# A recurrent mixer rewritten without a reciprocal, in pairs of blocks, with its gate weights as two ordinary weight tiles

## The chip, the cores and the metric

The kernel runs on one core of one Trainium2 chip. The metric is device microseconds of one execution. The kernel before takes 1469.25 us, the median of three runs from 1468.46 to 1470.31.

## The reference

Two layers of a decoder trunk for one prompt (16 learned tokens and 512 of its own) and eight samples of eight tokens. Layer 0 is stick-breaking attention beside a multi-scale pooling, layer 1 a recurrent block; each layer ends in a gated FFN with a convolution of width 3, and each half is followed by `x <- LN(alpha*x + f(x))`. The change lies in the recurrent block, with 1024 channels in 8 blocks of 128:

```
gate, rec = split(x @ lru_w_in)
xc        = causal depthwise conv of width 4 over rec, plus bias
gate_r    = sigmoid(xc @ w_a + b_a)           per block of 128 channels
gate_i    = sigmoid(xc @ w_x + b_x)
log_a     = -8 * gate_r * softplus(-lambda);  a = exp(log_a)
b         = sqrt(-expm1(2*log_a)) * gate_i * xc;   b[0] += a[0] * h0
h[t]      = a[t] * h[t-1] + b[t]              a scan over time
out       = (gelu(gate) * h) @ lru_w_out
```

## The kernel before

Activations lie with channels on partitions and all 592 tokens along the free axis: 528 of the prompt (`TP`), then 8 samples of 8. A product in full precision is three float32r matmuls: of high parts, of low part and high part, and the other way round (`mm3`, L121). So each weight tile is loaded by DMA into `wraw` (two buffers), copied on ScalarE to its high part and subtracted on VectorE or GpSimd to its low part (`split` at L98, `weights` at L105). `whl` tiles come in turn from two pools of three. Activations that feed matmuls are split in the same way: `ch`/`cl` of the convolution's result, `yh`/`yl` of the mixer's result, always copied on ScalarE and subtracted on GpSimd. Tokens are worked in two chunks of 296 (`CH`).

The recurrent mixer is written block by block. `rec_c` (L905) multiplies for `rec` and evacuates into `re`, `gate_c` (L918) for `gate` with gelu into `gt`. `conv4` (L929) makes `xc` in four steps on VectorE, a tensor_scalar and three products of two tensors, and splits it. `lru` (L949) loads and splits this block's 128x256 gate weights (`gr`, `wga`), multiplies (`pga`, 12 matmuls), takes sigmoids into `rg` and `ig`, and then works without an exponential. With t the Tanh of half the exponent's size, a = 2/(1+t) - 1, and the root is sqrt(t) * 2/(1+t):

```
act.activation(rg, rg, AF.Tanh, scale=sc4[:, i:i + 1])
dve.tensor_scalar(aa, rg, 1.0, None, op0=OP.add)
dve.reciprocal(aa, aa)
act.activation(rg, rg, AF.Sqrt)
```

The scan (L983) runs over all tokens at once. At each sample's first token a is set to 0 and a*h0 added to b, by three operations of 8 elements. `fin` (L989) multiplies by the gate and splits to `yh`/`yl`.

The string `ORDER` (L38) lists the pieces: r is `rec_c` and `conv4`, g is `gate_c`, B is `lru`, o one block of the first part of the output projection (`lru_out`, tiles `plo`, from the y of blocks 0 to 2). A block's `fin` follows when its B and its g are there. Five pieces (`seq`, L995) have their first chunk multiplied earlier, while the second chunk of the layer norm before is still being made. Behind the ORDER comes the second part of the projection (`Residual` with `w_lo1`, tiles `pr`, from the y of blocks 3 to 7, 15 matmuls for each of 8 output blocks and 2 chunks), whose statistics and norm lead into the second FFN.

Each engine runs its instructions in one fixed order. In this part a scheduler sets the orders when the program is built, from the order as written, its own cost model and the buffers that are free; so they do not stand in the source. Tiles with tag "e" (`et`, 8 buffers) hold `re`, `rt`, `rg`, `ig`, `aa` and `gt`; `blk` tiles (19) hold `xc` among others. TensorE's results go to six banks of PSUM (`pd`), which are free again when ScalarE has read them.

Of the kernel before, what the change touches and what calls it, by code (L numbers as in the profile page):

```python
# [10 lines left out]
F32 = mybir.dt.float32  # L11
# [8 lines left out]
KB = 8  # L20
# [17 lines left out]
ORDER = 'r0 r1 r2 g0 B0 r3 B1 g1 r4 B2 g2 r5 B3 g3 r6 B4 g4 r7 B5 g5 B6 g6 B7 g7 o0 o1 o2 o3 o4 o5 o6 o7'  # L38
# [6 lines left out]
HQ, EP = 19, 8  # L45
# [3 lines left out]
BW = 3 + TP + NS * 11  # L49

# [18 lines left out]
def trunk(ctx: ExitStack, tc: tile.TileContext, I, O):  # L69
# [35 lines left out]
    def weights(src, nk, le=None, parts=1, between=None):  # L105

        raw = wp.tile([128, 1024], F32, tag="wraw", name="wraw", bufs=2)
        wpool, tag = wcfg["pools"][wcfg["n"] % len(wcfg["pools"])]
        wcfg["n"] += 1
        w = wpool.tile([128, 2, 1024], F32R, tag=tag, name="whl")  # L110
        step = nk * 128 // parts
        for i in range(parts):
            wcfg["dma"].dma_start(raw[:, i * step:i * step + step], src[:, i * step:i * step + step])
# [804 lines left out]
    def gate_c(i, w, ci):  # L918
        lo, hi = CH[ci]
        p = pd("pgt", hi - lo)  # L920
        mm3(p, w, xh, xl, lo, hi, KB, 0, 4)
        yield
        mm3(p, w, xh, xl, lo, hi, KB, 4, 8)
        if ci == 0:
            gts[i] = et(f"gt{i}", n=T)
        act.activation(gts[i][:, lo:hi], p, AF.Gelu_apprx_tanh)
        yield

    def conv4(i):  # L929
# [10 lines left out]
        xc = blk(f"xc{i}")  # L940
        dve.scalar_tensor_tensor(xc[:, :TP], e[:, 3:3 + TP], cws[3], t[:, :TP], op0=OP.mult, op1=OP.add)
        tv = t[:, 3 + TP:3 + TP + NS * (TS + 3)].rearrange("p (s n) -> p s n", s=NS)[:, :, :TS]
        dve.scalar_tensor_tensor(xc[:, TP:].rearrange("p (s n) -> p s n", s=NS), ev[:, :, 3:], cws[3], tv,
                                 op0=OP.mult, op1=OP.add)
        ch, cl = pairA("c", i)
# [3 lines left out]
    def lru(i):  # L949
        xc, ch, cl = xcs.pop(i)  # L950
# [16 lines left out]
        aa = et(f"aa{i}", n=T)
# [210 lines left out]
```

## Time and profile before

| | us |
|---|---|
| median of three runs | 1469.25 |
| the profiled execution | 1470.56 |
| its span, first to last instruction | 1468.8 |
| busy: TensorE | 1371.5 (93%) |
| busy: VectorE | 816.1 (56%) |
| busy: ScalarE | 587.3 (40%) |
| busy: GpSimd | 451.2 (31%) |
| mean granted TensorE clock | 0.97 of full speed |

The profile is one execution, taken by the hardware profiler. PE is TensorE, DVE is VectorE, ACT is ScalarE, POOL is GpSimd. L949 is a line of the kernel. A share over the whole span mixes stages: attention up to some 390 us, the two FFNs, and the recurrent mixer from about 776 to 970 us. A granted clock of 1.00 is 2.4 GHz, the lower level is 1.2 GHz.

### The profile page before, as it was taken

The page shows a single profiled execution, that of the slowest core. Times are in us where ns is not written, and L with a number is a line of the kernel's source. Part 1 is how long each engine was busy: PE and PEld are TensorE (multiplying, and loading weights), DVE is VectorE, ACT ScalarE, POOL GpSimd, SP SyncE. Part 2 cuts the span into 40 slices and gives each one's busy share as a digit, 9 for nine tenths or more (in the row PEclk, how much of TensorE's full clock was granted, in tenths as well). Part 3 has the DMA queues.
Part 4 walks back from the last instruction along what each step waited for, and adds up shares of the span by engine and source line. Part 5 has one row for each costly group of instructions (what it writes and reads, how often), then busy time and mean ns, then how long its engine had stood idle before and what let it go on. Part 6 is the DMA issues. An engine that isn't in the chain of part 4 may idle for free.

```text
span 1468.8 us, 26738 instructions
## 1 busy us (share of the span) xinstructions
PE 1371.5 (93%) x10491; PEld 1294.3 (88%) x10491; DVE 816.1 (56%) x1220; ACT 587.3 (40%) x1083; POOL 451.2 (31%) x621
## 2 busy tenths in 40 slices
PE   8999798998999999999997787897999999999995
PEld 7988555798999999999997787886999999999994
DVE  4226676575743344334477699888734344433456
ACT  4333575444522233213245466735522133312333
POOL 3112220346320011102257656447531012101244
PEclk9999899999999999999998898998999999999997
DMA  9499887842422222222241210143222222222121
GB/s 311 169 373 372 308 286 259 302 135 87 129 73 87 86 73 87 79 80 79 67 120 58 62 65 28 28 121 115 73 91 82 87 81 78 87 87 87 57 90 65
DMA packets 78592, 183.74 MB, mean 125 GB/s; under 512 B 9458, under 2 KB 18291, under 8 KB 78467
## 3 DMA queue, kind: packets, MB, share of 16 engines
q1 hardware_dynamic: 75362, 170.77, 35.3%
q0 software_dynamic: 3104, 11.27, 2.1%
q8 instruction: 83, 1.36, 0.4%
q14 instruction: 43, 0.34, 0.1%
HBM read 176.38 MB, written 5.62 MB: 124 GB/s over the span
## 4 chain that ended last, share of the span: by engine, by line
PE 75%; DVE 14%; issue 4%; ACT 3%; POOL 2%; DMA 1%; SPq 0%; DVEq 0%; ACTq 0%; POOLq 0%
PE pv L127 19%; PE pg L127 18%; PE pdn L127 14%; PE pr L127 4%; PE pqk L127 3%; PE zs L640 2%; PE pv L415 2%; DVE r L251 2%; PE av L668 2%; DVE whl L101 2%; PE zp L517 1%; PE pu L127 1%; DVE r L250 1%; PE prc L127 1%; DVE r L209 1%
## 5 line engine op out<-in xcount | busy, mean ns | idle before, releaser
L100 ACT ACTIVATE whl<-wraw 128x1024 fp32r<-128x1024 f32 (+4 forms) x217 | 212.4, 981 | 338.9 <-PE pdn L127 150.6
L127 PE MATMUL pg<-xh,whl 128*128 128x296 f32 (+1 forms) x1408 | 293.0, 300 | 4.2 <-ACT xh L257 4.2
L101 DVE TENSOR_TENSOR whl<-wraw,whl 128x1024 fp32r<-128x1024 f32 (+3 forms) x198 | 234.9, 1187 | 102.2 <-ACT whl L100 101.6
L127 PE MATMUL pv<-xh,whl 128*128 128x296 f32 (+1 forms) x1408 | 290.2, 298 | 0.0
L127 PEld LDWEIGHTS pg<-xh,whl 128*128 128x128 f32 x1408 | 231.5, 191 | 4.8 <-ACT xh L257 4.4
L127 PEld LDWEIGHTS pv<-xh,whl 128*128 128x128 f32 x1408 | 229.0, 188 | 0.0
L127 PE MATMUL pg<-xl,whl 128*128 128x296 f32 (+1 forms) x704 | 210.7, 301 | 6.8 <-POOL xl L258 6.8
L127 PE MATMUL pv<-xl,whl 128*128 128x296 f32 (+1 forms) x704 | 209.1, 297 | 0.0
L127 PE MATMUL pdn<-fh,whl 128*128 128x296 f32 (+1 forms) x1024 | 207.7, 298 | 0.0
L101 POOL TENSOR_TENSOR fl<-f,fh 128x592 fp32r<-128x592 f32 (+1 forms) x44 | 82.7, 1879 | 273.1 <-ACT fh L100 273.1
L127 PEld LDWEIGHTS pdn<-fh,whl 128*128 128x128 f32 x1024 | 165.5, 188 | 0.0
L127 PE MATMUL pdn<-fl,whl 128*128 128x296 f32 (+1 forms) x512 | 151.7, 297 | 0.0
L127 PEld LDWEIGHTS pg<-xl,whl 128*128 128x128 f32 x704 | 133.8, 191 | 9.0 <-POOL xl L258 8.9
L127 PEld LDWEIGHTS pv<-xl,whl 128*128 128x128 f32 x704 | 133.0, 189 | 0.0
L807 DVE TENSOR_SCALAR gc<-ge,sm 128x608 f32<-128x608 f32 x44 | 26.2, 595 | 169.4 <-ACT ge L770 159.4
L801 POOL COPY fout<-ge 128x2 f32<-128x2 f32 x44 | 15.7, 358 | 326.1 <-ACT ge L767 326.0
L767 ACT ACTIVATE ge<-pg 128x296 f32<-128x296 f32 (+2 forms) x88 | 33.8, 386 | 157.2 <-PE pg L127 155.2
L127 PEld LDWEIGHTS pdn<-fl,whl 128*128 128x128 f32 x512 | 96.4, 189 | 0.0
L393 DVE TENSOR_TENSOR_SCAN kp<-kp,zero 128x256 f32<-128x256 f32 (+5 forms) x70 | 54.1, 774 | 73.7 <-ACT kp L392 73.2
L864 DVE SCALAR_TENSOR_TENSOR r<-r,pdn 128x296 f32<-128x296 f32 (+1 forms) x64 | 29.0, 459 | 118.0 <-PE pdn L127 118.0
L821 DVE TENSOR_TENSOR f<-gc,pv 128x296 f32<-128x296 f32 (+1 forms) x88 | 37.5, 426 | 99.6 <-PE pv L127 75.4
L127 PE MATMUL pr<-fh,whl 128*128 128x296 f32 (+1 forms) x384 | 79.4, 300 | 0.0
(263 smaller groups left out, 2726.9 us busy)
## 6 DMA issues: line engine op xcount, KB each, us to landing
ck<-in_ck SPq DMA_DIRECT2D x128, 256.0 KB, 5.1
cv<-in_cv SPq DMA_DIRECT2D x128, 256.0 KB, 5.2
wraw<-in_w_g SPq DMA_DIRECT2D x44, 512.0 KB, 3.3
wraw<-in_w_vv SPq DMA_DIRECT2D x44, 512.0 KB, 3.4
wraw<-in_w_d SPq DMA_DIRECT2D x32, 512.0 KB, 3.3
wraw<-in_w_d SPq DMA_DIRECT2D x26, 384.0 KB, 3.1
wraw<-in_w_lo SPq DMA_DIRECT2D x13, 320.0 KB, 3.0
wraw<-in_w_o POOLq DMA_DIRECT2D x8, 512.0 KB, 6.4
```

Source lines behind the costliest of these rows:

```text
L100: act.activation(h, src, AF.Copy)
L101: (le or dve).tensor_tensor(l, src, h.bitcast(F32), op=OP.subtract)
L127: pe.matmul(ps, lhsT=w[:, wi, s], rhs=x[k][:, lo:hi], start=(n == 0), stop=(n == 3 * nk - 1))
L251: dve.scalar_tensor_tensor(x, x, g, rs, op0=OP.mult, op1=OP.mult)
L393: dve.tensor_tensor_scan(kp[:, n - 1::-1], kp[:, n - 1::-1], zero.to_broadcast([128, n]), 1.0 if carry is None else carry, op0=OP.mult, op ...
L415: pe.matmul(p, lhsT=x[k][:, i * 128:i * 128 + n], rhs=w[k // 4][:, wi, s], start=(j == 0), stop=(j == 3 * KB - 1))
L640: pe.matmul(z[c * 32:c * 32 + 32, :256].rearrange("p (j n) -> p j n", j=2), lhsT=qb[b][:, c, r, :], rhs=kt[:, b, :, c * 128:c * 128 + 128] ...
L668: pe.matmul(av[c * 32:c * 32 + 32], lhsT=an[:, j * 128 + c * 32:j * 128 + c * 32 + 32], rhs=vt[:, :, j, c * 128:c * 128 + 128], start=(u = ...
L767: act.activation(e[:, k + lo:k + z], p[:, :z - lo], AF.Copy)
L807: dve.tensor_scalar(t[:, :n], e[:, :n], cws[0], smc("fcb", L * FB + j), op0=OP.mult, op1=OP.add)
L821: dve.tensor_tensor(f[:, lo:z], t[:, lo:z], p[:, :z - lo], op=OP.mult)
L864: dve.scalar_tensor_tensor(x, x, ALPHA if gi == 0 else 1.0, p, op0=OP.mult, op1=OP.add)
```

## The change

- The coefficient a is taken with Exp, and one correction step takes up Exp's error: with w from Exp and t from Tanh, nt = (w+1)t + (w-1), nt = (w+1)nt, a = w - nt/2. The root is sqrt(t) * (1+a). The reciprocal and its two tensor_scalars are gone; four 600-wide products of two tensors a block come in (L991 to L994 of the new file), and one Exp on ScalarE.
- The first step of the width-4 convolution goes from VectorE to ScalarE (an Identity activation with scale and bias, L944).
- Each sample has a column of its own for its start: tiles are 600 wide (`XW`), a is 0 there and b is h0. One memset and one copy of 8 elements replace the three operations at the starts; the gate product becomes two pieces (528 and 64 wide); `pga` is worked in two halves of 300.
- `lru` takes two blocks: all their sigmoids, then both Exp, both Tanh, then each block's rest.
- The gate weights of four blocks become one ordinary weight tile: w0 stands ahead of everything in ORDER, w1 ahead of r6. Eight small loads and splits go.
- ORDER is rewritten in pairs (B01, B23, B45, B67). `seq` has four r and one g where it had three r and two g. "e" tiles: 13 where there were 8. `xc` moves to an "e" tile, `gt` to a `blk` tile.

```
-ORDER = 'r0 r1 r2 g0 B0 r3 B1 g1 r4 B2 g2 r5 B3 g3 r6 B4 g4 r7 B5 g5 B6 g6 B7 g7 o0 ... o7'
+ORDER = 'w0 r0 r1 r2 r3 g0 B01 g1 r4 r5 g2 B23 g3 w1 r6 r7 g4 B45 g5 g6 B67 g7 o0 ... o7'
-HQ, EP = 19, 8
+HQ, EP = 19, 13
+XW = TP + NS * (1 + TS)
+CX = ((0, XW // 2), (XW // 2, XW))
...
-        dve.tensor_scalar(t[:, :n], e[:, :n], cws[0], smc("lcb", i), op0=OP.mult, op1=OP.add)
+        act.activation(t[:, :n], e[:, :n], AF.Identity, scale=cws[0], bias=smc("lcb", i))
...
-    def lru(i):
-        raw = w2.tile([128, 256], F32, tag="gr", name="gr", bufs=1)
-        sp.dma_start(raw, I["w_ga"][i])
-        wga = w2.tile([128, 2, 256], F32R, tag="wga", name="wga", bufs=1)
-        split(wga[:, 0], wga[:, 1], raw)
...
-        act.activation(rg, rg, AF.Tanh, scale=sc4[:, i:i + 1])
-        dve.tensor_scalar(aa, rg, 1.0, None, op0=OP.add)
-        dve.reciprocal(aa, aa)
-        act.activation(rg, rg, AF.Sqrt)
-        pool.tensor_tensor(ig, ig, xc, op=OP.mult)
-        dve.scalar_tensor_tensor(rg, rg, 2.0, aa, op0=OP.mult, op1=OP.mult)
-        dve.tensor_tensor(ig, ig, rg, op=OP.mult)
-        dve.tensor_scalar(aa, aa, 2.0, -1.0, op0=OP.mult, op1=OP.add)
...
+    def lru(ids):
...
+        for i in ids:
+            w = ws[i] = et(f"aa{i}", n=XW)
+            act.activation(w, rgs[i], AF.Exp, scale=sc8[:, i:i + 1])
+        for i in ids:
+            act.activation(rgs[i], rgs[i], AF.Tanh, scale=sc4[:, i:i + 1])
+        for i in ids:
+            w, rg, ig = ws[i], rgs[i], igs[i]
+            xc = xcs.pop(i)[0]
+            pool.tensor_tensor(ig, ig, xc, op=OP.mult)
+            t = et(f"nt{i}", n=XW)
+            dve.scalar_tensor_tensor(t, w, 1.0, rg, op0=OP.add, op1=OP.mult)
+            dve.scalar_tensor_tensor(t, w, -1.0, t, op0=OP.add, op1=OP.add)
+            dve.scalar_tensor_tensor(t, w, 1.0, t, op0=OP.add, op1=OP.mult)
+            dve.scalar_tensor_tensor(w, t, -0.5, w, op0=OP.mult, op1=OP.add)
+            act.activation(rg, rg, AF.Sqrt)
+            dve.scalar_tensor_tensor(rg, w, 1.0, rg, op0=OP.add, op1=OP.mult)
+            dve.tensor_tensor(ig, ig, rg, op=OP.mult)
+            dve.memset(starts(w), 0.0)
+            dve.tensor_copy(starts(ig), smr("h0")[:, i * 8:i * 8 + 8].rearrange("p (s n) -> p s n", n=1))
+            dve.tensor_tensor_scan(ig, w, ig, 0.0, op0=OP.mult, op1=OP.add)
...
+        elif k == "w":
+            wgas[i] = weights(I["w_ga"][i * 4:i * 4 + 4].rearrange("b p n -> p b n"), KB)
```

What the scheduler makes of it is seen in the queues. The first place is ScalarE between the sigmoids and the Sqrt. Before, this is block 1 (`rg_9434` and `ig_9435` are its gates, `re_9533` is block 4):

```order
L964 ACT_TABLE_LOAD
L964 ACTIVATE rg_9434<-pga,sm 128x296 x2
L100 ACTIVATE wga<-gr 128x256
L966 ACTIVATE rg_9434<-rg_9434,sc_8907 128x592
L926 ACT_TABLE_LOAD
L926 ACTIVATE gt_9125<-pgt 128x296
L100 ACTIVATE whl<-wraw 128x1024
L964 ACT_TABLE_LOAD
L964 ACTIVATE ig_9435<-pga,sm 128x296 x2
L767 ACTIVATE re_9533<-prc 128x296
L970 ACT_TABLE_LOAD
L970 ACTIVATE rg_9434<-rg_9434 128x592
```

After the change, between the pairs 01 and 23 (`ch_9654` is of block 5, `rg_9716` and `ig_9717` of block 2, `rg_9738` and `ig_9739` of block 3, `gt_9688` of block 2); behind these rows stand a weight split, a table load, the Exp of block 3 and the Tanh of block 2:

```order
L102 ACTIVATE ch_9654<-xc_9650 128x600
L933 ACTIVATE gt_9688<-pgt 128x296
L102 ACTIVATE whl<-wraw 128x1024
L978 ACT_TABLE_LOAD
L978 ACTIVATE rg_9716<-pga,sm 128x300 x2
L978 ACTIVATE ig_9717<-pga,sm 128x300 x2
L978 ACTIVATE rg_9738<-pga,sm 128x300 x2
L978 ACTIVATE ig_9739<-pga,sm 128x300
L983 ACT_TABLE_LOAD
L983 ACTIVATE aa_9760<-rg_9716,sc_8937 128x600
L978 ACT_TABLE_LOAD
L978 ACTIVATE ig_9739<-pga,sm 128x300
```

The sigmoids of two blocks stand together, but the last one comes behind a first Exp, and the copy of block 5's convolution stands ahead of them all. The queue has 28 table loads between the mixer's first gelu and its last in the old program, and 32 in the new one.

The second place is VectorE at the same point. Before, it begins with the scan of block 0 (L983, which this list names like any product) and the reciprocal of block 1 (`aa_9457`); `ig_9313` is block 0, `rt_9566` and `re_9533` block 4, `rg_9434` block 1:

```order
L983 SCALAR_TENSOR_TENSOR ig_9313<-aa_9335,ig_9313 128x592
L969 RECIPROCAL aa_9457<-aa_9457 128x592
L991 TENSOR_TENSOR ig_9313<-ig_9313,gt_9078 128x592
L937 TENSOR_SCALAR rt_9566<-re_9533,sm 128x616
L101 TENSOR_TENSOR wga<-gr,wga 128x256
L972 SCALAR_TENSOR_TENSOR rg_9434<-rg_9434,aa_9457 128x592
L938 SCALAR_TENSOR_TENSOR rt_9566<-re_9533,sm,rt_9566 128x616
L973 TENSOR_TENSOR ig_9435<-ig_9435,rg_9434 128x592
L974 TENSOR_SCALAR aa_9457<-aa_9457 128x592
L939 SCALAR_TENSOR_TENSOR rt_9566<-re_9533,sm,rt_9566 128x616
```

After the change, `rt_9646` and `xc_9650` are of block 5, `nt_9767` of block 2, `nt_9781` of block 3; ahead of these rows stand the last gate product of block 1 and the convolution of block 4:

```order
L945 SCALAR_TENSOR_TENSOR rt_9646<-re_9613,sm,rt_9646 128x616
L946 SCALAR_TENSOR_TENSOR rt_9646<-re_9613,sm,rt_9646 128x616
L949 SCALAR_TENSOR_TENSOR xc_9650<-re_9613,sm,rt_9646 128x528
L951 SCALAR_TENSOR_TENSOR xc_9650<-re_9613,sm,rt_9646 128x8x8
L991 SCALAR_TENSOR_TENSOR nt_9767<-aa_9760,rg_9716 128x600
L992 SCALAR_TENSOR_TENSOR nt_9767<-aa_9760,nt_9767 128x600
L991 SCALAR_TENSOR_TENSOR nt_9781<-aa_9762,rg_9738 128x600
L993 SCALAR_TENSOR_TENSOR nt_9767<-aa_9760,nt_9767 128x600
```

Where operations of two or three blocks alternated, the convolutions of a pair are now followed directly by the chain of the pair before it in the order of blocks, which starts from ScalarE's results.

## Rows read from the trace of the kernel before

**Rows 1.** Windows: us, busy us of each engine (instructions), PEclk, DMA share, GB/s.
```profile
400.00:740.00 340.00, 340.00 (x2501) 340.00 (x2500) 131.37 (x194) 89.51 (x136) 50.24 (x86) 1.00 0.25 79
815.00:838.00 23.00, 15.03 (x90) 14.51 (x88) 18.79 (x16) 10.47 (x20) 17.30 (x13) 0.78 0.21 68
838.00:963.00 125.00, 103.33 (x683) 99.09 (x682) 120.14 (x119) 84.42 (x131) 70.82 (x83) 0.93 0.16 47
963.00:1010.00 47.00, 42.26 (x294) 40.80 (x293) 37.48 (x67) 21.19 (x36) 23.05 (x22) 0.96 0.42 124
```

**Rows 2.** VectorE's groups by form, 765 to 980 us: busy us, mean ns | idle before.
```profile
L969 DVE RECIPROCAL aa<-aa 128x592 f32<-128x592 f32 x8 | 30.8, 3846 | 0.1
...
L937 DVE TENSOR_SCALAR rt<-re,sm 128x616 f32<-128x616 f32 x8 | 11.3, 1414 | 9.6 <-ACT re L770 9.6
...
L974 DVE TENSOR_SCALAR aa<-aa 128x592 f32<-128x592 f32 x8 | 9.3, 1161 | 0.0
```

**Rows 3.** Source lines: duration ns min/median/max, first and last start us, forms.
```profile
L969 DVE RECIPROCAL aa<-aa x8: 3820/3852/3853, 838.9 to 947.2; 128x592 f32<-128x592 f32 x8
...
L983 DVE TENSOR_TENSOR_SCAN ig<-aa,ig x8: 1327/1414/2647, 853.6 to 959.1; 128x592 f32<-128x592 f32 x8
...
L991 DVE TENSOR_TENSOR ig<-ig,gt x8: 710/762/2972, 858.7 to 962.6; 128x592 f32<-128x592 f32 x8
```

**Rows 4.** VectorE's timeline in the mixer: start us, us, instruction [idle before].
```profile
815.06 0.60 DVE L937 TENSOR_SCALAR rt<-re,sm 128x616 f32<-128x616 f32 x1 [9.63 <-ACT re L770]
...
860.83 0.76 DVE L972 SCALAR_TENSOR_TENSOR rg<-rg,aa 128x592 f32<-128x592 f32 x1
861.52 2.03 DVE L938 SCALAR_TENSOR_TENSOR rt<-re,sm,rt 128x616 f32<-128x616 f32 x1
...
867.08 2.98 DVE L939 SCALAR_TENSOR_TENSOR rt<-re,sm,rt 128x616 f32<-128x616 f32 x1
...
870.45 0.75 DVE L941 SCALAR_TENSOR_TENSOR xc<-re,sm,rt 128x528 f32<-128x528 f32 x1
...
871.32 3.84 DVE L969 RECIPROCAL aa<-aa 128x592 f32<-128x592 f32 x1
```

**Rows 5.** GpSimd's timeline, 855 to 868 us, columns as in rows 4.
```profile
857.04 2.39 POOL L101 TENSOR_TENSOR whl<-wraw,whl 128x1024 fp32r<-128x1024 f32 x1 [0.81 <-ACT whl L100]
860.87 2.02 POOL L101 TENSOR_TENSOR yl<-ig,yh 128x592 fp32r<-128x592 f32 x1 [1.44 <-ACT yh L100]
...
865.36 1.47 POOL L971 TENSOR_TENSOR ig<-ig,xc 128x592 f32<-128x592 f32 x1 [0.48 <-ACT ig L964]
866.79 2.61 POOL L101 TENSOR_TENSOR whl<-wraw,whl 128x1024 fp32r<-128x1024 f32 x1
```

**Rows 6.** ScalarE's timeline in the mixer, columns as in rows 4.
```profile
833.62 1.28 ACT L964 ACT_TABLE_LOAD   x1
834.92 0.90 ACT L964 ACTIVATE rg<-pga,sm 128x296 f32<-128x296 f32 x2
835.71 0.91 ACT L964 ACTIVATE ig<-pga,sm 128x296 f32<-128x296 f32 x2
...
836.79 0.80 ACT L966 ACTIVATE rg<-rg,sc 128x592 f32<-128x592 f32 x1
837.48 1.07 ACT L100 ACTIVATE whl<-wraw 128x1024 fp32r<-128x1024 f32 x1
838.42 0.43 ACT L767 ACTIVATE re<-prc 128x296 f32<-128x296 f32 x1
...
860.09 0.70 ACT L100 ACTIVATE yh<-ig 128x592 fp32r<-128x592 f32 x1 [2.88 <-DVE ig L991]
860.70 0.69 ACT L100 ACTIVATE ch<-xc 128x592 fp32r<-128x592 f32 x1
```

**Rows 7.** The projection behind the mixer: its matmuls' tile, and the chain that ended last.
```profile
L127 PE MATMUL pr<-yh,whl x160: 287/297/837, 969.0 to 1008.7; 128*128 128x282 f32 x80, 128*128 128x296 f32 x80
...
972.37 3.23 DMA wraw<-in_w_lo
```

More of the change, by code (lines that the diff above doesn't have):

```diff
@@ L112, in weights @@
         for i in range(parts):
-            wcfg["dma"].dma_start(raw[:, i * step:i * step + step], src[:, i * step:i * step + step])
+            if len(src.shape) == 3:
+                wcfg["dma"].dma_start(raw[:, :nk * 128].rearrange("p (b n) -> p b n", b=src.shape[1]), src)
+            else:
+                wcfg["dma"].dma_start(raw[:, i * step:i * step + step], src[:, i * step:i * step + step])
         for i in range(parts):
@@ L899, in trunk @@
     dve.tensor_scalar(sc4, w1[:, 0], 8.0, None, op0=OP.mult)
+    sc8 = con.tile([128, KB], F32, name="sc8")
+    dve.tensor_scalar(sc8, w1[:, 0], -16.0, None, op0=OP.mult)
     xh, xl = res.xh, res.xl
     es, gts, xcs, hss = {}, {}, {}, {}
-    ys, gated = {}, set()
+    ys, gated, wgas = {}, set(), {}
     def rec_c(i, w, ci):
@@ L936, in conv4 @@
         t = et(f"rt{i}")
-        dve.tensor_scalar(t[:, :n], e[:, :n], cws[0], smc("lcb", i), op0=OP.mult, op1=OP.add)
+        act.activation(t[:, :n], e[:, :n], AF.Identity, scale=cws[0], bias=smc("lcb", i))
         dve.scalar_tensor_tensor(t[:, :n], e[:, 1:n + 1], cws[1], t[:, :n], op0=OP.mult, op1=OP.add)
         dve.scalar_tensor_tensor(t[:, :n], e[:, 2:n + 2], cws[2], t[:, :n], op0=OP.mult, op1=OP.add)
-        xc = blk(f"xc{i}")
+        xc = et(f"xc{i}", n=XW)
+        pool.memset(starts(xc), 0.0)
@@ new lines, in starts, with tokens @@
+    def starts(t):
+        return t[:, TP:XW].rearrange("p (s n) -> p s n", s=NS)[:, :, 0:1]
+    def tokens(t):
+        return t[:, TP:XW].rearrange("p (s n) -> p s n", s=NS)[:, :, 1:]
+    def lru(ids):
+        rgs, igs, ws = {}, {}, {}
+        for i in ids:
+            wga, c0 = wgas[i // 4], i % 4 * 256
+            xc, ch, cl = xcs[i]
+            rgs[i], igs[i] = et(f"rg{i}", n=XW), et(f"ig{i}", n=XW)
+            for k, (dst, bn) in enumerate(((rgs[i], "lba"), (igs[i], "lbx"))):
+                for lo, hi in CX:
+                    p = pd("pga", hi - lo)
+                    j = 0
+                    for wi, x in ((0, ch), (0, cl), (1, ch)):
+                        pe.matmul(p, lhsT=wga[:, wi, c0 + k * 128:c0 + k * 128 + 128], rhs=x[:, lo:hi],
+                                  start=(j == 0), stop=(j == 2))
+                        j += 1
+                    act.activation(dst[:, lo:hi], p, AF.Sigmoid, bias=smc(bn, i))
+        for i in ids:
[3 more added lines that the diff above has]
+            act.activation(rgs[i], rgs[i], AF.Tanh, scale=sc4[:, i:i + 1])
+        for i in ids:
+            w, rg, ig = ws[i], rgs[i], igs[i]
[12 more added lines that the diff above has]
+            dve.tensor_tensor_scan(ig, w, ig, 0.0, op0=OP.mult, op1=OP.add)
+            pool.tensor_copy(lho[:, i, 0:1], ig[:, TP - 1:TP])
+            pool.tensor_copy(lho[:, i, 1:].rearrange("p (s n) -> p s n", n=1), tokens(ig)[:, :, TS - 1:])
+            hss[i] = ig
@@ L989, in fin @@
     def fin(i):
-        hs, gt = hss.pop(i), gts.pop(i)
-        dve.tensor_tensor(hs, hs, gt, op=OP.mult)
+        hs, y = hss.pop(i), gts.pop(i)
+        dve.tensor_tensor(y[:, :TP], y[:, :TP], hs[:, :TP], op=OP.mult)
+        yv = y[:, TP:].rearrange("p (s n) -> p s n", s=NS)
+        dve.tensor_tensor(yv, yv, tokens(hs), op=OP.mult)
         h, l = ys[i] = pairA("y", i)
-        split(h, l, hs, pool)
-    seq = [("r", 0), ("r", 1), ("g", 0), ("g", 1), ("r", 2)]
+        split(h, l, y, pool)
@@ L996, in trunk @@
+    seq = [("r", 0), ("r", 1), ("r", 2), ("r", 3), ("g", 0)]
     ws = {}
@@ L1020, in trunk @@
     out = lru_out()
-    for k, i in ((x[0], int(x[1])) for x in ORDER.split()):
+    for k, ids in ((x[0], [int(c) for c in x[1:]]) for x in ORDER.split()):
+        i = ids[0]
         if k == "B":
-            lru(i)
+            lru(ids)
+        elif k == "w":
+            wgas[i] = weights(I["w_ga"][i * 4:i * 4 + 4].rearrange("b p n -> p b n"), KB)
         elif k == "o":
```

39 lines of the change are left out of this document (7 added, 32 removed).

## The prediction

> **What bounds the kernel now.** I read the busy time by stage first, then VectorE's groups in the recurrent mixer, then the timelines of VectorE, GpSimd and ScalarE there, and last the projection behind it.
>
> In the FFN before the mixer TensorE is busy for the whole of a 340 us stretch, with 2501 matmuls, so a matmul costs 0.136 us at a granted clock of 1.00, and nothing that the change does there can show [rows 1]. In the mixer it is otherwise. From 838 to 963 us VectorE is busy 120.1 of 125 us, ScalarE 84.4 and GpSimd 70.8, while TensorE issues 683 matmuls, 93 us of work at 0.136. VectorE sets the pace, and at most some 32 us of waiting can be had there.
>
> The reciprocal runs from 838.9 (block 0) to 947.2 us (block 7) and the last gate product starts at 962.6 and takes 0.76 [rows 3]: 124.5 us from the first reciprocal to the last product, 15.6 a block. The reader should see two things in VectorE's rows. The reciprocal costs a steady 3.82 to 3.85 us, and a tensor_scalar that can take 0.45 averages 1.16 to 1.41 [rows 2, 3]. The second is not arithmetic: the 616-wide product of two tensors at 867.08 takes 2.98 us while a weight split of 2.61 us runs on GpSimd, the one at 861.52 takes 2.03 while the split of y (2.02 us from 860.87) runs, and a product of the same kind just before takes 0.69 to the next start [rows 4, 5]. While GpSimd subtracts two tensors, VectorE's next two-tensor operation stands still. So their times add, except beside a reciprocal, which is not stretched [rows 3].
>
> **What the change removes.** On VectorE, per block, the reciprocal, the first convolution step (now ScalarE's), two tensor_scalars and three small operations at the sample starts. The three large groups were busy 30.8, 11.3 and 9.3 us [rows 2], 51 us.
>
> **What it adds there.** Four 600-wide products of two tensors a block (nt three times, aa once). None is in the trace; the nearest is L972 at 0.69 unstalled [rows 4], so 32 x 0.69 = 22 us, and up to 2.98 each if all stall. The gate product becomes two pieces. By arithmetic alone VectorE wins about 28 us. But the reciprocal was the one operation under which GpSimd could work for nothing, and its replacements stall.
>
> **ScalarE.** It gains eight Identity passes and eight Exp passes. Neither is in the trace; the Tanh beside them takes 0.69 (836.79 to 837.48) and a plain copy 0.61 [rows 6]; I take 0.69, bounds 0.6 to 0.9. Its program has 32 table loads in the mixer where it had 28, so the pairs share none. A load costs 1.30 from start to the next activation, two sigmoids 0.79, a weight split 0.94 [rows 6]. The Trainium skill (ScalarE: Activation LUTs, What ACT_TABLE_LOAD costs) counts a drain of 1.38 us on top, 2.66 for every switch; by that the 16 loads that I find on the path below would add 22 us and the time would be about 1504. The trace has the next activation 1.30 after the load, so the sum keeps 1.30 and the 1504 gets no chance.
>
> **What the order does.** This decides it. Before, VectorE's queue mixed blocks: behind the reciprocal of block 1 stood block 0's product, block 4's convolution and block 1's rest, so while ScalarE worked on one block VectorE had another. Now the queue runs: chain of a pair, both next convolutions, then directly nt of the next pair. And ScalarE's queue has the copy ch of block 5, which waits for VectorE's xc5, ahead of every sigmoid of blocks 2 and 3, whose Exp and Tanh nt waits for. So VectorE stands while ScalarE does this, one after the other, none of it beside the convolutions.
>
> Stand of VectorE between pairs 01 and 23: ch 0.6, gelu 0.4 (as a sigmoid), two weight splits 1.9, four table loads 5.2, eight sigmoids 3.2, two Exp and a Tanh 2.1: **13.3 us**. Between 23 and 45, with one short split: **11.5 us**. Between 45 and 67 there are no convolutions, and only from yh4 on does ScalarE follow VectorE: yh4, yh5, three loads, a sigmoid, two Exp, a Tanh: **8 us**.
>
> VectorE's own phases, unstalled. Per block: conv 2 x 0.7 + 0.87 (870.45 to 871.32 is both pieces of the last step, [rows 4]), five products 3.5, one more 0.7, the scan 1.3 [rows 3], the gate product 0.8, small ones 0.2. A pair with two convolutions: 17.5; pair 01 has a 1024-wide weight split more, 1.2 by width: 18.7. GpSimd's subtractions inside the phase, at 2.39 for a weight split and 1.46 for a block [rows 5]: two of each for pair 01, 7.7 us; about 8 for pair 23, 4.4 for 45, 6 for 67. In pair 23 VectorE also waits for Tanh and Sqrt of block 3 (1.0 each, table loads for gelu stand between) and for rt7, behind yh3 and a split on ScalarE (2.3): 4.3.
>
> - Pair 01 to 23: 18.7 + 7.7 + 13.3 = 39.7
> - 23 to 45: 17.5 + 4.3 + 8 + 11.5 = 41.3
> - 45 to 67: 12.2 (two chains without convolutions, 13.0, less the last gate product, beside which yh4 already runs) + 4.4 + 8 = 24.6
> - 67 to the last gate product: 13.0, sixteen additions from plo at half the width (0.4 each, 6.4), four 640-wide splits by width (0.75 each, 3), 2 of waits, 6 of GpSimd = 30.4
>
> Together 136.0 us where it took 124.5: **+11.5**.
>
> **The start.** Block 0's convolution began at 815.06 after 9.6 us idle [rows 4]. Now block 0's rt follows a weight split on ScalarE (+0.9). Four convolutions (9 us) stand ahead of the chain instead of three, and between them GpSimd has three weight splits of 2.39 and three splits of 1.46: xc3 at about 840.4. Then ch3, a split, three sigmoids, four loads, two Exp, a sigmoid, gelu, Tanh: 10.8 us. The chain starts at 851.2, not 838.9: **+12.3**, or +6 if no subtraction falls between.
>
> **The end.** The last product ends 24 us later, at 987.2; y's split of block 7 (0.6 on ScalarE, 1.46 on GpSimd) is done at 989.3. Before, the projection's first matmul was at 969.0 and its last at 1008.7, 39.7 us for 240 matmuls (the row's 160 with high parts and 80 with low), 32.8 us of work; the other 7 went to loads such as the 3.23 us one [rows 7]. Now five blocks of its weights can be split while VectorE finishes, and 12 of the first 15 matmuls need no block 7. I give back 6 and 1.6: 989.3 + 32.8 + 1 - 1.6 = 1021.5, against 1008.7: **+12.8 us**. Behind that the program is as before.
>
> **Costed at nothing:** the two gate-weight tiles. They are asked for ahead of g1 and of r6, each lands in some 3 us like its neighbours [rows 7], and one split replaces four. If one came late, TensorE and the whole pair would wait 3 to 4 us. The eight zero columns add 1.4% to the pga matmuls, on an engine with 32 us to spare.
>
> **The sum.** The profiled execution took 1470.56 us, 1.3 above the median of the three runs, 1469.25; +12.8 gives 1483.4 for it and 1482 against the median.
>
> **Rivals.**
>
> *Faster: GpSimd fits into VectorE's stands.* The sum has about 32 us of GpSimd's subtractions standing in VectorE's way (6 at the start, 7.7, 8, 4.4, 6). The stands of 13.3 and 11.5 us are long enough for most of it. If it falls there, the lighter arithmetic shows: with 20 us of the 32 gone, 1462. It decides at 13 us. For it: VectorE's idle time is where a waiting GpSimd would run. Against: the y splits and the next weight splits are released by VectorE's own last operations, in the phase, as at 860.87 and 866.79 [rows 5].
>
> *No change.* About half of that, or TensorE's projection catching up more than 7 us: within 1466 to 1472.
>
> *Slower still: TensorE becomes late too.* During the stands TensorE fills its six result banks and stops. After such gaps the granted clock was 0.78 on average from 815 to 838 [rows 1], a mix of the two levels, 1.2 and 2.4 GHz. At the lower one 24 matmuls take 3.3 us longer, and the gelu of block 3, ahead of Tanh 3 on ScalarE, waits for just those. Three pairs: +10, 1492.
>
> **How the numbers follow.** My forecast 0.56, slower still 0.13, no change 0.10, faster 0.21. A change of 0.2% (2.9 us) is about what a measurement of this kernel can tell. The price bounds alone, all of GpSimd's work hidden or all of it plus the slow clock, reach from 1450 (1482 less 32) to 1502 (twice the slow clock's 10 more); the range leaves out the outer fifths of that: 1460 to 1494. The forecast's own range is 1474 to 1489. Slower 0.69, same 0.10, faster 0.21.
>
> **What would show it.** In the new profile nt0 starts near 851; VectorE idles 11 to 14 us ahead of nt2 and nt4, released by ScalarE's Tanh; the scans come in pairs some 40 us apart; ScalarE has 32 loads at 1.28; the projection's first block ends after 988 and it has no 3 us gaps. I am wrong if VectorE stays over 90% busy from the first nt to the last product, or if the products L991 to L994 average under 0.75 us: then the lock is the step that failed. If the stands are under 8 us, the order is.

## The result, and the profile after

The changed kernel takes 1482.1 us (median of five runs, 1477.9 to 1483.1) where the kernel before takes 1470.3 in the same session: a ratio of 1.0070, with a 95% interval of 1.0054 to 1.0087. It is slower, and the forecast of 1482.0 fits. The experiments show that one of its reasons was wrong all the same, and the trace that two of its terms were.

| the profiled execution | before | after |
|---|---|---|
| its time, us | 1470.56 | 1480.58 |
| its span, us | 1468.8 | 1478.8 |
| VectorE busy, us | 816.1 | 774.6 |
| ScalarE busy, us | 587.3 | 604.7 |
| first product or reciprocal step of the mixer, us | 838.4 | 851.5 |
| end of the last gate product, us | 963.4 | 980.6 |
| first matmul of the FFN behind, us | 1013.2 | 1028.4 |

First the windows of after: us, busy us of each engine (instructions), granted clock, DMA share, GB/s.

```profile
838.00:963.00 125.00, 98.99 (x656) 96.86 (x656) 72.20 (x96) 95.69 (x136) 73.52 (x74) 0.87 0.13 42
963.00:1010.00 47.00, 43.30 (x313) 41.91 (x311) 36.01 (x66) 20.01 (x34) 24.11 (x25) 1.00 0.44 128
1010.00:1030.00 20.00, 5.33 (x34) 5.04 (x33) 19.85 (x32) 9.78 (x19) 11.65 (x12) 0.69 0.38 112
```

VectorE, the third pair of numbers, falls from 120.1 [rows 1] to 72.2 of the 125 us, and the last gate product ends 17 us later. Part of the fall is work that now lies behind 963 us; over the whole execution VectorE is busy 41.5 us less. Where an engine loses that much work and the stage ends later, it has stopped being what sets the end. VectorE's timeline of after says what it waits for (start, duration, instruction, idle before and its releaser):

```profile
817.49 2.31 DVE L945 SCALAR_TENSOR_TENSOR rt<-re,sm,rt 128x616 f32<-128x616 f32 x1 [11.72 <-ACT rt L944]
...
851.50 1.48 DVE L991 SCALAR_TENSOR_TENSOR nt<-aa,rg 128x600 f32<-128x600 f32 x2 [11.52 <-ACT rg L985]
...
890.93 0.78 DVE L991 SCALAR_TENSOR_TENSOR nt<-aa,rg 128x600 f32<-128x600 f32 x1 [14.07 <-ACT rg L985]
...
931.05 1.53 DVE L991 SCALAR_TENSOR_TENSOR nt<-aa,rg 128x600 f32<-128x600 f32 x2 [12.20 <-ACT rg L985]
...
955.22 0.78 DVE L991 SCALAR_TENSOR_TENSOR nt<-aa,rg 128x600 f32<-128x600 f32 x1 [9.80 <-ACT rg L985]
...
980.36 0.21 DVE L1010 TENSOR_TENSOR gt<-gt,ig 128x64 f32<-128x64 f32 x1
```

Each pair opens with 10 to 14 us of idle, released by ScalarE's Tanh. ScalarE's timeline of after ahead of 890.93, same columns, shows what it does meanwhile:

```profile
876.95 0.70 ACT L102 ACTIVATE ch<-xc 128x600 fp32r<-128x600 f32 x1 [3.93 <-DVE xc L951]
877.56 0.40 ACT L933 ACTIVATE gt<-pgt 128x296 f32<-128x296 f32 x1
877.86 1.05 ACT L102 ACTIVATE whl<-wraw 128x1024 fp32r<-128x1024 f32 x1
878.92 1.28 ACT L978 ACT_TABLE_LOAD   x1
880.22 0.91 ACT L978 ACTIVATE rg<-pga,sm 128x300 f32<-128x300 f32 x2
...
883.15 1.28 ACT L983 ACT_TABLE_LOAD   x1
884.45 0.80 ACT L983 ACTIVATE aa<-rg,sc 128x600 f32<-128x600 f32 x1
885.26 1.28 ACT L978 ACT_TABLE_LOAD   x1
886.56 0.51 ACT L978 ACTIVATE ig<-pga,sm 128x300 f32<-128x300 f32 x1
...
888.04 1.28 ACT L983 ACT_TABLE_LOAD   x1
889.33 0.80 ACT L983 ACTIVATE aa<-rg,sc 128x600 f32<-128x600 f32 x1
890.03 0.78 ACT L985 ACTIVATE rg<-rg,sc 128x600 f32<-128x600 f32 x1
```

From the copy ch of block 5 to Tanh it runs without a gap for 13.1 us, and four table loads are 5.2 of them: a Sigmoid, the first Exp, back for the last half of the last sigmoid, Exp again. The Tanh behind Exp needs no load. This last half was not late. The last of its matmuls, in TensorE's timeline, ends at 882.65 us, 0.5 us ahead of the load for the first Exp, and in the other three pairs it is 0.8 to 1.3 us ahead. It stands behind that Exp because the order was fixed when the program was built.

```profile
882.20 0.45 PE L975 MATMUL pga<-ch,whl 128*128 128x300 f32 x1
```

### The profile page after: what moved, and what is told of

It reads as the page before. It is cut to its first block, busy times and chain, and to the rows that moved or that the text cites. A ratio compares the mean times of both kernels' runs of the same rounds, so it can differ in the third digit from the quotient of the medians.

```text
span 1478.8 us, 26717 instructions
## 1 busy us (share of the span) xinstructions
PE 1371.1 (93%) x10491; PEld 1293.9 (87%) x10491; DVE 774.6 (52%) x1215; ACT 604.7 (41%) x1097; POOL 458.9 (31%) x629
## 4 chain that ended last, share of the span: by engine, by line
PE 75%; DVE 10%; ACT 6%; issue 4%; POOL 3%; DMA 2%; SPq 0%; DVEq 0%; ACTq 0%; POOLq 0%
PE pv L132 19%; PE pg L132 19%; PE pdn L132 14%; PE pr L132 5%; PE pqk L132 3%; PE zs L645 2%; PE av L673 2%; PE pv L420 2%; PE zp L522 1%; PE pu L132 1%; DVE r L256 1%; PE prc L132 1%; DVE r L214 1%; DMA wraw<-in_w_lo 1%; DVE r L255 1%
## 5 line engine op out<-in xcount | busy, mean ns | idle before, releaser
L132 PE MATMUL pg<-xh,whl 128*128 128x296 f32 (+1 forms) x1408 | 293.9, 300 | 14.7 <-ACT xh L262 14.7
```

What stands on the lines that cost most here:

```text
L132: pe.matmul(ps, lhsT=w[:, wi, s], rhs=x[k][:, lo:hi], start=(n == 0), stop=(n == 3 * nk - 1))
```

## The experiments

Each kernel ran beside the kernel before on the same chip; ratios are to that kernel, with their 95% intervals. The first four take the change apart.

**The gate step cut in two** (ratio 1.0118, 1.0099 to 1.0137; 1489.2 us).

```
-  ... r2 r3 g0 B01 g1 r4 r5 g2 B23 g3 w1 r6 r7 ...
+  ... r2 r3 g0 B01 g1 C01 B23 r4 r5 g2 w1 C23 B45 g3 r6 r7 ...
```

B is now the sigmoids, Exp and Tanh, C the products and scans.

> The changed kernel with the gate step cut in two: the sigmoids, Exp and Tanh of a pair are issued ahead of the convolutions of the next pair, the products and scans behind them. Arithmetic, pairs and tiles are unchanged. My theory (VectorE stands 14.07, 12.20 and 9.80 us behind ScalarE because the copy of the next convolution's result is queued ahead of a pair's sigmoids): the three stands fall under 5 us each, the last gate product comes 15 to 30 us earlier than 980.6 us, and the time is 1452 to 1466, faster than both kernels, though ScalarE has two table loads more. Rival (VectorE's added products collide with GpSimd, or ScalarE itself is the bound): the idle time moves inside the chains, the last product stays after 972 us and the time is 1474 or more.

A miss. VectorE's timeline of this kernel, then a row of TensorE's timeline and its matmuls for the second part of the projection:

```profile
880.02 4.03 DVE L994 SCALAR_TENSOR_TENSOR nt<-aa,rg 128x600 f32<-128x600 f32 x2
...
914.99 0.71 DVE L1011 TENSOR_TENSOR gt<-gt,ig 128x528 f32<-128x528 f32 x1 [11.28 <-issue]
...
925.10 1.47 DVE L994 SCALAR_TENSOR_TENSOR nt<-aa,rg 128x600 f32<-128x600 f32 x2
...
955.48 0.78 DVE L994 SCALAR_TENSOR_TENSOR nt<-aa,rg 128x600 f32<-128x600 f32 x1 [10.59 <-ACT rg L986]
```
```profile
973.53 0.58 PE L132 MATMUL plo<-yh,whl 128*128 128x282 f32 x1 [3.25 <-DVE r L1039]
...
L132 PE MATMUL pr<-yh,whl x160: 287/297/522, 987.3 to 1025.0; 128*128 128x282 f32 x80, 128*128 128x296 f32 x80
```

The stands ahead of nt2 and nt4 are gone (no idle at 880.02 and 925.10), as wanted, and the time is worse. VectorE now stands 11.28 us ahead of block 3's gate product. The row names no releaser, but block 3's gelu ends 0.1 us before. This gelu comes in halves: the first is 5 us late for TensorE's matmuls (903.42), the second stands at 914.48 behind the next pair's sigmoids and Exp. And ScalarE changes tables 34 times in the mixer instead of 32, Sigmoid and Sqrt in turn.

Even so the last gate product ends at 975.5 us, 5.1 earlier than in after, where the theory wanted 15 to 30. The time is lost behind it, to TensorE: at 973.53 its matmuls for the first part of the projection (`plo`) still wait 3.25 us for VectorE's additions, and the second part (`pr`) starts at 987.3, where it starts at 976.6 in after. The FFN's first matmul comes at 1030.2 instead of 1028.4, and the FFN then takes 6.3 us more (see *The end* below). So VectorE's stands could not be taken off by themselves: a part came back as another stand, and the rest was lost behind the mixer.

**The old arithmetic in pairs** (1.0041, 1.0023 to 1.0059; 1476.2 us).

```
-ORDER = 'r0 r1 r2 g0 B0 r3 B1 g1 r4 B2 ...'
+ORDER = 'r0 r1 r2 r3 g0 B01 g1 r4 r5 g2 B23 ...'
-HQ, EP = 19, 8
+HQ, EP = 19, 12
```

> The kernel before with its old arithmetic (reciprocal, first convolution step on VectorE, gate weights by block), but in pairs and in the new written order, with 12 buffers in the pool of the large tiles. My theory (order costs, arithmetic gains): it has the stands and the late start without the lighter arithmetic, so it is slower than the changed kernel by some of the 40 us that VectorE's work differs by: 1490 to 1515. Rival (the new arithmetic, with its products and its Exp, is what costs): 1465 to 1480, as fast as the changed kernel or faster.

The rival's range. Pairs cost the old arithmetic some 6 us. The new arithmetic, with the rest of the change, costs another 6 by the medians and 4 by the ratios in the same pairs, though its VectorE has so much less to do. Its ScalarE has more: 32 table loads in the mixer where this kernel has 24, and with Exp between them a pair's first product waits for both blocks' sigmoids. Here a block's reciprocal starts when its own Tanh is done, the first at 843.9 us instead of 851.5.

**The new arithmetic without pairs** (1.0014, 1.0001 to 1.0026; 1473.9 us).

```
-ORDER = 'w0 r0 r1 r2 r3 g0 B01 g1 r4 r5 g2 B23 g3 w1 ...'
+ORDER = 'w0 r0 r1 r2 g0 B0 r3 B1 g1 r4 B2 g2 r5 B3 g3 w1 ...'
```

> The changed kernel's arithmetic, tiles and buffers, but one block at a time in the order of before (the two gate-weight tiles placed ahead of the first block and ahead of the seventh convolution). It has 5 table loads more than the changed kernel. My theory: a chain of 8.8 us of VectorE's own work per block no longer covers the 10 to 12 us that ScalarE needs from sigmoid to Tanh, so VectorE stands at every block, for shorter times, and starts earlier (its first product near 840 instead of 851.5): 1465 to 1485. Rival (the pairs themselves are the loss): VectorE is busy over 85% from the first to the last product and the time is under 1460. Rival (table loads set the time): 5 x 1.3 us more than the changed kernel, 1487 or more.

As expected, in time and in kind. Its window and VectorE's group of the first product (busy, mean ns, idle before):

```profile
838.00:963.00 125.00, 98.75 (x636) 95.24 (x636) 104.55 (x112) 101.91 (x142) 77.84 (x86) 0.90 0.14 47
```
```profile
L991 DVE SCALAR_TENSOR_TENSOR nt<-aa,rg 128x600 f32<-128x600 f32 x8 | 11.5, 1443 | 22.7 <-ACT rg L985 22.7
```

ScalarE is busy 101.9 of 125 us, 17 more than before [rows 1], with 37 table loads in the mixer where it had 28. Even in the old order the lighter arithmetic is worth nothing.

**The first convolution step back on VectorE** (1.0066, 1.0046 to 1.0087; 1481.3 us).

```
-        act.activation(t[:, :n], e[:, :n], AF.Identity, scale=cws[0], bias=smc("lcb", i))
+        dve.tensor_scalar(t[:, :n], e[:, :n], cws[0], smc("lcb", i), op0=OP.mult, op1=OP.add)
```

> The changed kernel with the first convolution step back on VectorE. My theory: VectorE takes on 8 steps of 0.45 to 1.4 us, in the phases that set the pace, and ScalarE loses 8 passes of 0.7 us, of which only the first and the last lie on the path: 3 to 8 us slower than the changed kernel, 1485 to 1490. Rival (ScalarE's extra pass ahead of each convolution is what makes the change slower): faster than the changed kernel by 3 us or more, 1479 or less.

Neither: the same time as the changed kernel. VectorE has eight steps more, of 1.37 us on average, and ScalarE eight passes of 0.9 us less but two table loads more. So the moved step is no cause of the slower time; which of the two engines decides, this kernel can't tell.

The next four ask what on ScalarE it is.

**Blocks of a pair one after the other** (1.0108, 1.0088 to 1.0129; 1486.7 us): the order of the change with B0 B1 for B01, and so on.

> The changed kernel with everything in its place (four convolutions ahead, pairs side by side in the written order), but the gate step called for one block at a time: the sigmoids, Exp, Tanh and products of a pair's first block stand ahead of the sigmoids of its second. My theory, mended after the first four runs: a pair's first product waits for the sigmoids and Exp passes of both blocks and four table loads; taken singly it starts earlier (844 to 848 instead of 851.5, the stands 8 to 10 us instead of 10 to 14), so 3 to 7 us faster than the changed kernel: 1475 to 1479, though it has 2 loads more. Rival (the grouping within a pair is not it, the four convolutions ahead and their place are): within 2 us of the changed kernel, 1480 to 1485.

A miss. The chain does start earlier, at 841.2 us, and the pairs then take 42.5, 42.5 and 25.2 us from first product to first product, longer than the 39.4, 40.1 and 24.2 of after. This kernel has two loads more in the mixer, and waits inside the pair that the grouped one has not. Grouping two blocks shortens the pairs, then, and delays their start, and in this execution (1482.05 us, the fastest of this kernel) the two about cancel: the last gate product ends at 978.2 us, 2.4 earlier than in after, and the FFN's first matmul comes 4.0 earlier, at 1024.4. The loss lies in the FFN, which takes 455.6 us from there to the end of the span where after takes 450.4 (*The end*). No trace shows what makes the median 4.6 us slower than this execution.

**Sigmoids as tanh, in pairs** (0.9968, 0.9957 to 0.9980; 1466.5 us).

```
-   act.activation(dst[:, lo:hi], p, AF.Sigmoid, bias=smc(bn, i))
+   act.activation(dst[:, lo:hi], p, AF.Tanh, scale=0.5, bias=lbh[:, k, i:i + 1])
...
-   pool.tensor_tensor(ig, ig, xc, op=OP.mult)
+   dve.scalar_tensor_tensor(ig, ig, 1.0, xc, op0=OP.add, op1=OP.mult)
...
-   act.activation(rg, rg, AF.Sqrt)
+   act.activation(rg, rg, AF.Sqrt, scale=0.25)
```

> The changed kernel with the two gates' sigmoids computed as tanh of half the argument, so that they share a table with Exp's and gelu's neighbours: 28 table loads in the program instead of 40. The missing half and one go into the scale and bias of the Exp, Tanh and Sqrt passes, and the product with xc becomes a two-tensor product with an added one on VectorE instead of GpSimd (eight of 0.78 us more there). My theory (ScalarE's chain from the first sigmoid to Tanh sets VectorE's stands, and table loads are some 4 of them each): 12 loads of 1.30 us less, up to 15.6 us, less 3 to 6 for the product: 1466 to 1475, faster than the changed kernel. Rival (the loads hide behind what ScalarE waits for, the convolutions and GpSimd): 1479 or more.

As expected, at the strong end: 15.6 us faster than the changed kernel by the medians and 15.0 by the ratios, where 12 loads of 1.30 us make 15.6; and faster than the kernel before. The same stretch of ScalarE's timeline, ahead of nt2:

```profile
873.03 0.70 ACT L102 ACTIVATE ch<-xc 128x600 fp32r<-128x600 f32 x1 [4.49 <-DVE xc L954]
...
876.95 0.54 ACT L981 ACTIVATE ig<-pga,lbh 128x300 f32<-128x300 f32 x1
877.50 1.28 ACT L986 ACT_TABLE_LOAD   x1
878.80 0.89 ACT L986 ACTIVATE aa<-rg,sc 128x600 f32<-128x600 f32 x1
879.59 0.49 ACT L981 ACTIVATE ig<-pga,lbh 128x300 f32<-128x300 f32 x1
...
880.93 0.88 ACT L986 ACTIVATE aa<-rg,sc 128x600 f32<-128x600 f32 x1
881.71 0.88 ACT L988 ACTIVATE rg<-rg,sc 128x600 f32<-128x600 f32 x1
...
883.90 0.42 ACT L936 ACTIVATE gt<-pgt 128x296 f32<-128x296 f32 x1
884.21 0.88 ACT L988 ACTIVATE rg<-rg,sc 128x600 f32<-128x600 f32 x1
```

The last half of the gate stands behind the first Exp as before, but it no longer changes the table: one load instead of four, 8.7 us from ch to Tanh instead of 13.1. In VectorE's timeline the first product comes 5.3 us earlier than in after (846.23; 1.4 of them lie ahead of the first convolution), the three pairs are 3.0, 3.9 and 3.9 us shorter, the last stretch 0.5 longer: together 15.6. In the Trainium skill (ScalarE: Activation LUTs, Table sets: the hidden batching unit) tables are loaded in sets, tanh is in Exp's and in Sigmoid's, and activations are to be batched by set, not by function. These rows agree for Exp's table and [rows 6] for Sigmoid's, and the gelu here has tanh beside it too: block 3's Tanh, at 884.21, runs right behind a gelu without a load.

**The same, blocks one at a time** (0.9970, 0.9957 to 0.9983; 1465.6 us): the order and start of before.

> The same with the blocks taken one at a time in the order of before: 36 table loads where the unpaired kernel has 45. My theory (there ScalarE is the engine that is busy without a gap, and VectorE waits 22.7 us in all for its Tanh): 9 loads of 1.30 us less, 11.7 us, less some of the 6 us that VectorE gains: 1462 to 1470, faster than both kernels. Rival (the cycle from VectorE's gate product through the convolution copy to the next Tanh is made of waits, not of ScalarE's work): 1473 or more.

As expected: 8.2 us faster than the unpaired kernel by the medians, 6.5 by the ratios, with 9 loads fewer. And the order no longer matters: pairs and single blocks take the same time here (0.9968 and 0.9970), where beside the sigmoids the pairs cost 8 us (1.0070 against 1.0014).

**The gate-weight tiles alone** (0.9972, 0.9960 to 0.9985; 1467.8 us).

```
-        raw = w2.tile([128, 256], F32, tag="gr", name="gr", bufs=1)
-        sp.dma_start(raw, I["w_ga"][i])
...
+        wga, c0 = wgas[i // 4], i % 4 * 256
```

> The kernel before with one part of the change alone: the gate weights as two weight tiles of four blocks, the first asked for ahead of the first convolution, the second ahead of the seventh. VectorE loses eight splits of 128x256 (0.4 to 1.7 us each). My theory (the weights are no cause): 1464 to 1472. Rival (a tile held for four blocks takes one of six slots from the matmuls, and TensorE starts later): 1475 or more.

As expected, and the one part of the change that pays by itself, 3 us by the medians and 4 by the ratios. So the new arithmetic in the old order costs 6 (1.0014 against 0.9972); the sample columns and the buffer counts changed together with it and were not tried alone.

Then two controls and two attempts at more.

**The product with xc on VectorE, alone** (1.0062, 1.0044 to 1.0080; 1480.9 us): `pool.tensor_tensor(ig, ig, xc, ...)` becomes `dve.tensor_tensor`.

> The changed kernel with one thing that the tanh version also did, alone: the product of the input gate with xc on VectorE instead of GpSimd. Sigmoids and all 40 table loads stay. My theory (the table loads are what the tanh version gained by): no gain, 1480 to 1487. Rival (it gained by taking eight two-tensor passes of 1.5 us off GpSimd, out of VectorE's way): 1475 or less.

As expected, 1.2 us under the changed kernel, less than the intervals. So the tanh version owes its gain to the loads, and eight products more on VectorE, taken from GpSimd, cost nothing.

**A mixed order** (0.9952, 0.9936 to 0.9967; 1463.8 us).

```
-ORDER = 'w0 r0 r1 r2 r3 g0 B01 g1 r4 r5 g2 B23 ...'
+ORDER = 'w0 r0 r1 r2 g0 B0 r3 B1 g1 r4 r5 g2 B23 ...'
```

> The tanh version in pairs, but with the start of before: three convolutions ahead, blocks 0 and 1 taken singly, pairs from block 2 on; 30 table loads in the program. My theory (a late start is lost for good): the first product comes at 834 to 838 us instead of 846.2 and most of that is kept, 1457 to 1463. Rival (with the loads gone TensorE sets the pace, 108 matmuls or 14.7 us a block at 0.136, and what starts earlier waits for it): 1464 to 1469, the same as the tanh version in pairs.

Just outside my range and at the rival's edge. It is the fastest by its median, but its interval overlaps that of the tanh version in pairs, and its trace speaks for the rival in part: the first product comes 7 us earlier, at 839.1, and block 2's at the same 882.7 us as in the tanh version in pairs. The traced execution is one of its slower ones, though (1467.0 us), and the mixer's first matmul comes 3.9 us later in it. Counted from that matmul, the lead is 11.0 us at the first product, 3.9 at block 2's and 2.0 at the end of the last gate product. Most of the early start is lost, not all. To what, no run here settles.

**The cut gate step with tanh** (1.0012, 0.9998 to 1.0026; 1474.1 us): gates moved ahead (`... B01 g1 C01 B23 g2 r4 r5 g3 C23 w1 B45 g4 r6 r7 g5 ...`).

> The tanh version with the gate step cut in two as in the first of these experiments, and the gate matmuls of blocks 2, 3 and 5 moved ahead of the next pair's gate step, where VectorE had stood 11.28 us for a gelu; 32 table loads in the program. My theory (there the stand moved to the gelu because TensorE was given the gate step first, and four loads of Sigmoid and Sqrt in turn lay between): 1460 to 1470. Rival (VectorE's stands return wherever GpSimd's subtractions and its products meet, whatever the order): 1475 or more.

A miss between the two: better than without tanh by 15 us, no match for the plain pairs. VectorE stands 9.2 us for the Identity pass of block 6 in it.

**Two products less** (1.0058, 1.0039 to 1.0078; 1481.0 us).

```
-            dve.scalar_tensor_tensor(t, w, -1.0, t, op0=OP.add, op1=OP.add)
-            dve.scalar_tensor_tensor(t, w, 1.0, t, op0=OP.add, op1=OP.mult)
```

> The changed kernel with two of the three products of nt left out (the polynomial that takes the place of the reciprocal is cut short): 16 products of 0.78 us less on VectorE, the same 40 table loads. My theory (a pair's time is a sum, VectorE's phase and then ScalarE's, none beside the other): 16 starts of 0.70 us less, some 11 us, 1469 to 1474. Rival (VectorE has time to spare since its share fell to 72 of 125 us, and what it does in it costs nothing): 1479 to 1484.

This kernel leaves out two of the three products that make nt, so it computes something else; it serves for the time alone. My theory falls, the rival holds: 11 us of VectorE's phases taken away move the time by 1 (1.8 by the ratios), less than the intervals. Where they went, in VectorE's timeline of this kernel:

```profile
885.66 0.78 DVE L991 SCALAR_TENSOR_TENSOR nt<-aa,rg 128x600 f32<-128x600 f32 x1 [13.99 <-ACT rg L985]
...
888.08 0.78 DVE L991 SCALAR_TENSOR_TENSOR nt<-aa,rg 128x600 f32<-128x600 f32 x1 [0.74 <-ACT rg L985]
890.10 0.78 DVE L994 SCALAR_TENSOR_TENSOR rg<-aa,rg 128x600 f32<-128x600 f32 x1 [1.24 <-ACT rg L993]
...
894.79 1.07 DVE L994 SCALAR_TENSOR_TENSOR rg<-aa,rg 128x600 f32<-128x600 f32 x1 [2.50 <-ACT rg L993]
...
909.82 2.69 DVE L945 SCALAR_TENSOR_TENSOR rt<-re,sm,rt 128x616 f32<-128x616 f32 x1 [2.93 <-ACT rt L944]
```

VectorE waits inside the pair instead, for ScalarE's Sqrt and Identity; in pair 01 only 0.3 us of wait is new, but the two convolutions take 10.7 us where they took 9.7. Pairs 01 and 23 take 38.3 and 41.4 us, 79.7 together where after takes 79.6, and pair 45 takes 25.4 for 24.2; only the last stretch, which no pair follows, is 6 us shorter. So the mixer does get 4.5 us shorter from its first product on, and the FFN takes this back: its first matmul comes 9.8 us earlier than in after, the end of the span only 4.7 (*The end*). (The profiled execution is the fastest of this kernel's runs, 1475.8 us; 4.1 us of its lead lie ahead of the first convolution.)

## Why the prediction was right, and where it was not

**The start: right.** nt0 was forecast at 851.2 and begins at 851.50; the table loads are 32 and follow at 1.30 us. Four of them stand on the path to the first product of each of the four pairs, 16 as the prediction counts; the terms of its sum hold 15.

**The pairs: right in length, wrong in what makes it.** Forecast 39.7, 41.3 and 24.6 us, measured 39.4, 40.1 and 24.2, with stands of 14.07, 12.20 and 9.80 for 13.3, 11.5 and 8. The failed step is the sum itself, VectorE's phase plus ScalarE's stand, and with it "by arithmetic alone VectorE wins about 28 us", which the stands were to use up. VectorE's busy time did fall, by 41.5 us, but there was nothing to win by it once the new form was in: two products a block less on VectorE, or one more, leave the time within 2 us. A pair is a chain through both engines. ScalarE's list has no gap in the stand, but ahead of it ScalarE itself waits 3.93 us for VectorE's convolution (at 876.95), and what VectorE saves among its products it waits for Sqrt and Identity. What could be taken out of the chain were table loads, priced in the sum as part of the stands: 12 fewer gave 15.6 us. The Trainium skill (ScalarE: Activation LUTs, What ACT_TABLE_LOAD costs) has 2.66 us for a switch, which would have made that 32; the measurement decides for 1.30.

**GpSimd in VectorE's way: the size about right, the place wrong.** VectorE's groups of after (busy, mean ns):

```profile
L949 DVE SCALAR_TENSOR_TENSOR xc<-re,sm,rt 128x528 f32<-128x528 f32 x8 | 13.6, 1701 | 0.1
L946 DVE SCALAR_TENSOR_TENSOR rt<-re,sm,rt 128x616 f32<-128x616 f32 x8 | 13.1, 1647 | 0.1
...
L997 DVE TENSOR_TENSOR ig<-ig,rg 128x600 f32<-128x600 f32 x8 | 9.5, 1208 | 0.0
...
L992 DVE SCALAR_TENSOR_TENSOR nt<-aa,nt 128x600 f32<-128x600 f32 x8 | 6.1, 778 | 0.1
```

The text said that the lock was the failed step if L991 to L994 averaged under 0.75 us. They average 0.78, all unstalled: the threshold was set too near the plain price to tell. It is the convolutions that stretch (their fastest take 0.76 and 0.83) and the product at L997. Against their fastest, the convolution steps are busy some 21 us longer, and the products at L996 and L997 some 5 longer than at 0.78: 26 us, where the sum has 32.

**The end: wrong twice, and the errors nearly cancel.** From nt6 to the last gate product 30.4 us were forecast and 25.4 came, so the last product ends at 980.6 and not 987.2. For the projection +12.8 us were forecast, its end at 1021.5 and "behind that the program is as before". Its last matmul and the first of the FFN in after, then the FFN's first in before and in the kernel with two products less:

```profile
1013.44 0.30 PE L132 MATMUL pr<-yh,whl 128*128 128x296 f32 x1
1028.41 0.84 PE L132 MATMUL pg<-xh,whl 128*128 128x282 f32 x2 [14.67 <-ACT xh L262]
```
```profile
1013.18 1.55 PE L127 MATMUL pg<-xh,whl 128*128 128x282 f32 x5 [4.17 <-ACT xh L257]
```
```profile
1018.62 1.55 PE L132 MATMUL pg<-xh,whl 128*128 128x282 f32 x5 [4.85 <-ACT xh L262]
```

It ends only 4.7 us later than before [rows 7], and TensorE then idles 14.7 us for the norm, where it idled 4.2; in the window from 1010 to 1030 it is busy 5.3 of 20 us. The sign "the projection's first block ends after 988" fails with it: VectorE reads that block at 984.8. The failed step is that TensorE's projection sets the end. What does in after is the way from the last gate product through the sums and the norm to the FFN: 49.8 us before, 47.8 after, and between 46 and 55 in every other kernel (at 55 in the gate step cut in two, where the projection was late). The FFN so starts 15.2 us later; its first 30 us then hold 203 matmuls where before held 178, some 3.4 us at 0.136, and of the 15.2 us 10.0 are left at the end of the span. The fourteen traces fall into two groups by this: where TensorE idles 12.8 to 18.0 us for the norm, the span ends 450 to 454 us after the FFN's first matmul, and where it idles 4.2 to 5.1, it ends 455 to 457 after it. So part of a late start of the FFN is made up behind it, and the kernel with two products less loses there 5.1 of the 9.8 us by which its FFN starts earlier. The forecast had no such term, and its total fits in part by luck.

**The rivals.** "Faster" asked whether GpSimd fits into the stands; VectorE's work, lengthened by it or not, turned out not to decide. "Slower still" had the clock right and its effect wrong: TensorE is granted 0.87 from 838 to 963 us where it had 0.93 [rows 1], but the pairs are no longer than forecast without that. The range's upper end does not follow from its own rule, which gives 1492 and not 1494; the result lies far inside both.

## What to carry to other kernels

When work is taken off the busiest engine, ask which engine's list is next in length before pricing the gain: here VectorE gave up 41.5 us and ScalarE, which got the new passes and their table loads, held it up at every pair. Count the table loads of the built order, not the functions of the source; one activation that this order puts behind a function of another table costs two more of them, and expressing it by a function that the neighbours' table already holds removes them. Follow a saved microsecond to the end of the span: the stage behind can take it back. And a sum that meets the measured length does not show what makes it up: leave out one term and see.

## What I had not expected

A GpSimd split of 128x1024, 2.39 us in [rows 5], took 5.16 us (from 856.32) while VectorE ran its products back to back. For the first part of it not they but it waited: the products go on at 1.47 us for two. Only the last two, at 858.45, take 3.67. VectorE's own weight split comes behind them, at 862.06, and a weight load that the profile shows ScalarE standing 8.65 us for, until 867.67, was issued when that split had ended, at 863.29.

```profile
856.32 5.16 POOL L103 TENSOR_TENSOR whl<-wraw,whl 128x1024 fp32r<-128x1024 f32 x1 [7.71 <-ACT whl L102]
```
```profile
857.06 1.47 DVE L996 SCALAR_TENSOR_TENSOR rg<-aa,rg 128x600 f32<-128x600 f32 x2
858.45 3.67 DVE L997 TENSOR_TENSOR ig<-ig,rg 128x600 f32<-128x600 f32 x2
...
862.06 1.21 DVE L103 TENSOR_TENSOR whl<-wraw,whl 128x1024 fp32r<-128x1024 f32 x1
```
```profile
867.67 1.06 ACT L102 ACTIVATE whl<-wraw 128x1024 fp32r<-128x1024 f32 x1 [8.65 <-DMA wraw<-in_w_gate]
```

Before, a reciprocal came every 15.5 us [rows 3], and from its first product to that of block 6 the tanh version in pairs takes 15.5 a block too. TensorE's 108 matmuls for a block are 14.7 us at 0.136, so it may be the next limit. Between the first products of blocks 4 and 6 it is busy for 19.65 of 20.25 us there, at a granted clock of 1.00:

```profile
918.87:939.12 20.25, 19.65 (x145) 19.41 (x143) 15.92 (x25) 16.93 (x28) 8.12 (x9) 1.00 0.07 20
```

Ahead of that it is not (26.85 of 36.46 us between the first products of blocks 0 and 2), so for the mixer as a whole this is argued, and no run here shows it.
